# Two-layer encoder trunk on one core: the gate halves' spacing in V's weight tiles, and the ninth weight tile's role at the end of V

## The chip, the core and the metric

The kernel runs on one core of one Trainium2 chip. The metric is the device time of one execution in microseconds (us); of several runs the median is given. TensorE is called PE in the profile, its weight loads PEld, VectorE DVE, ScalarE ACT, GpSimd POOL and the engine that issues most transfers SP.

## What is computed

A sequence of 256 tokens plus 16 meta tokens (272 columns here, 1024 features) goes through two layers. Each has a token mixer (a gated recurrence in layer 0, a convolution module in layer 1) and then the part that takes nearly all the time, a PEER channel mixer:

```python
def peer_block(xc, w_query, sub_keys, expert_u, expert_v):
    ...
    expert = idx1 * PEER_N_KEYS + idx2          # 16 experts of 16384 for each head and token
    g = jax.nn.softmax(s.astype(jnp.float32), axis=-1).astype(xc.dtype)
    u = expert_u[expert]
    act = jax.nn.gelu(jnp.einsum('chkd,cd->chk', u, xc))
    v = expert_v[expert]
    return jnp.einsum('chk,chkd->cd', g * act, v)
```

After each mixer stands a layer norm. All of it is in float32.

## The kernel before

Most tokens take the PEER mixer densely: all 16384 experts are computed for them, as 128 tiles of 128 experts, and gates that are zero for experts not chosen weight the result. A stage "U" makes the activations (240 columns), a stage "V" multiplies the gated activations with the 128 tiles of `peer_v` and adds them up in eight PSUM banks `acc0` to `acc7`, one for each 128 features. V works on n = 208 columns in layer 0 and n = 192 in layer 1. The few other tokens draw single rows of the tables by indirect transfers (`rows`) in the background.

To keep float32 precision, each operand is split into a high part `hi` in a shorter format and the rest `lo`. For a tile of V, SP loads 512 KB (`raw<-peer_v`), ACT makes `hi` (line 154), DVE makes `lo` (line 161), and PE multiplies. The gates of four tiles (`JG = 4`) are split into one tile `w` by `weights`: ACT writes the high half, DVE the low half (lines 270 and 273). In it the two halves of one tile's gates lie side by side, each `T0` = 272 numbers wide, of which the first n are used. So one matmul with the weights `hi` takes both halves in one instruction (line 771: n columns, a jump, n columns, 416 or 384 in all), and one with the weights `lo` takes the high half alone (line 775). A full tile has eight of each. Two `w` tiles alternate; in the built program they begin at bytes 60640 and 69344 of each partition, both 224 above a multiple of 256.

The last four of the 128 tiles of V come as four half tiles, so that the norm after V can begin on the first 512 features while the others are still multiplied. `halves(q, h)` loads the columns of half h of two tiles (two transfers of 256 KB) and splits them. `finish_block(b)` finishes the features of bank b, and needs `halves(0, 0)` and `halves(1, 0)` for banks 0 to 3, `halves(0, 1)` and `halves(1, 1)` for banks 4 to 7. In layer 0 it is called by `collect`, which also norms, in layer 1 by `finish`, which writes the output. `take` (lines 841 and 842) adds the banks' first part to the residual `xr` on DVE.

Nine weight tiles of 4 KB per partition are shared by everything: four for `raw`, two for `hi`, two for `lo`, and a ninth, `spare`. `stream` decides who gets it by the flag `self.fifth`: where that is true, every fifth `raw` goes into it (five load tiles, two `hi`); where it is false, every third `hi` does (four load tiles, three `hi`). `u_store` sets it to true, and `peer` to false just before the half tiles. A tile can be written again once its last reader is done.

The order on each engine is set at build time by a scheduler that follows the waits of the program: an instruction that needs no buffer to come free can be placed ahead of one written earlier that does. At run time each engine, and SP's queue, works strictly in that order.

## Time and profile before

| | us |
|---|---|
| median of 3 runs | 1774.01 (1772.1 to 1779.39) |
| the profiled execution | 1777.1 |
| its span, first to last instruction | 1775.3 |
| PE busy | 1724.0 (97%) |
| DVE busy | 1511.7 (85%) |
| ACT busy | 901.1 (51%) |
| POOL busy | 625.0 (35%) |

The stage V of layer 0 runs from about 546 to 862 us of the span, its norm to about 888; V of layer 1 runs from about 1442 to 1740, and its four half tiles and the output to the end. In a view of the profile in order of time (the timeline), a row has the start and the time of a run of equal instructions, the engine, the line, what is written from what, how many, and in brackets how long the engine was idle before and what released it. The windows view gives, for each stretch, the engines' busy time, the clock granted to TensorE as a share of full speed, the share of busy DMA engines and GB/s.

### The profile page before, as it was taken

Reading aid. Unit: us, or ns where it says so; the run is one execution under the profiler, and the core shown is the slowest. Engines: PE = TensorE matmul, PEld = TensorE weight load, DVE = VectorE, ACT = ScalarE, POOL = GpSimd, SP = SyncE. Lnnn points to the kernel's source line nnn. Section 1 sums busy time; section 2 is a strip of 40 time slices with the busy share of each in tenths; the row PEclk is TensorE's granted clock in tenths of the full one; section 3 lists DMA queues with packets and bytes.
Section 4 is the critical chain, followed back from the end, with each engine's and each line's share of the span. In section 5 each row is a group of like instructions: output and inputs, shape, how many; then the busy total and the mean of one; then the engine's idle time right before and its main releaser. Section 6 shows DMA issues by size and latency. Waiting matters only on the chain.

```text
span 1775.3 us, 34693 instructions
## 1 busy us (share of the span) xinstructions
PE 1724.0 (97%) x13436; PEld 1676.6 (94%) x13436; DVE 1511.7 (85%) x2821; ACT 901.1 (51%) x1489; POOL 625.0 (35%) x424
## 2 busy tenths in 40 slices
PE   8999999999999999999998999999999999999995
PEld 7899999999999999999887899999999999999995
DVE  7786998899997889887799769978898978889865
ACT  6554444544445555885432645455444455555551
POOL 1101992111202556752000017922113137677300
PEclk9999999999999999999999999999999999999997
DMA  5545668866657999999441366579666679999982
GB/s 202 166 144 167 191 206 274 300 211 203 222 185 267 338 350 351 356 360 317 149 153 50 107 196 172 194 260 319 222 198 222 194 221 328 347 344 352 342 285 84
DMA packets 126022, 423.83 MB, mean 239 GB/s; under 512 B 20768, under 2 KB 21920, under 8 KB 125728
## 3 DMA queue, kind: packets, MB, share of 16 engines
q1 hardware_dynamic: 96272, 324.04, 55.3%
q0 software_dynamic: 29584, 97.58, 15.0%
q8 instruction: 105, 1.72, 0.4%
q14 instruction: 61, 0.50, 0.1%
HBM read 411.35 MB, written 10.20 MB: 237 GB/s over the span
## 4 chain that ended last, share of the span: by engine, by line
PE 78%; DVE 11%; DMA 4%; issue 3%; POOL 2%; ACT 2%; POOLq 0%; DVEq 0%; SPq 0%; ACTq 0%
PE u L189 42%; PE acc L771 17%; PE acc L775 11%; DMA rows<-peer_v,ids 4%; PE u L225 3%; DVE cy L1279 2%; DVE odd L1279 2%; DVE lo L161 1%; PE g L696 1%; PE g L697 1%; PE sps L587 1%; PE acc L810 1%; ACT hi L154 1%; DMA own<-own 1%; DVE x L372 1%
## 5 line engine op out<-in xcount | busy, mean ns | idle before, releaser
L154 ACT ACTIVATE hi<-raw 128x1024 fp32r<-128x1024 f32 x556 | 588.4, 1060 | 570.6 <-PE acc L771 211.5
L161 DVE TENSOR_TENSOR lo<-raw,hi 128x1024 fp32r<-128x1024 f32 x488 | 595.2, 1223 | 149.2 <-ACT hi L154 140.6
L189 PE MATMUL u<-xs,hi 128*128 128x240 f32 (+2 forms) x4544 | 568.7, 277 | 2.0 <-ACT hi L154 1.4
L189 PEld LDWEIGHTS u<-xs,hi 128*128 128x128 f32 x4544 | 537.5, 189 | 3.1 <-ACT hi L154 1.6
L771 PE MATMUL acc<-w,hi 128*128 128x416 f32 (+1 forms) x1984 | 410.6, 349 | 1.8 <-DVE w L273 1.8
L771 PEld LDWEIGHTS acc<-w,hi 128*128 128x128 f32 x1984 | 348.0, 189 | 3.5 <-DVE w L273 2.2
L1064 POOL DMA_INDIRECT rows<-peer_v,ids x128 | 206.5, 1613 | 320.8 <-DVE few_out L1105 170.2
L189 PE MATMUL u<-xs,lo 128*128 128x240 f32 (+2 forms) x2272 | 308.2, 276 | 4.1 <-POOL lo L161 3.4
L189 PEld LDWEIGHTS u<-xs,lo 128*128 128x128 f32 x2272 | 280.6, 189 | 6.1 <-POOL lo L161 5.0
L775 PEld LDWEIGHTS acc<-w,lo 128*128 128x128 f32 x2048 | 267.1, 192 | 10.3 <-DVE lo L161 8.5
L775 PE MATMUL acc<-w,lo 128*128 128x208 f32 (+1 forms) x2048 | 270.0, 273 | 6.0 <-DVE lo L161 3.5
L161 POOL TENSOR_TENSOR lo<-raw,hi 128x1024 fp32r<-128x1024 f32 x68 | 176.8, 2616 | 103.1 <-ACT hi L154 62.2
L1105 DVE SCALAR_TENSOR_TENSOR few_out<-rows,act,few_out 128x1024 f32<-128x1024 f32 x120 | 153.7, 1281 | 18.5 <-DMA rows<-peer_v,ids 18.0
L1064 POOL DMA_INDIRECT rows<-u_rows,ids x48 | 61.4, 1280 | 178.5 <-DVE rows L1071 138.8
L1081 POOL DMA_INDIRECT act<-own,turn x80 | 111.1, 1389 | 27.5 <-issue 18.6
L225 PE MATMUL u<-x,raw 128*128 128x272 f32 x480 | 114.2, 398 | 5.0 <-DMA x<-h 5.0
L225 PEld LDWEIGHTS u<-x,raw 128*128 128x128 f32 x480 | 92.6, 193 | 24.4 <-DMA raw<-w_in 5.0
L703 ACT ACTIVATE act_b<-g 128x488 f32<-128x488 f32 (+39 forms) x50 | 19.4, 388 | 123.7 <-DVE act_b L665 97.2
L380 POOL TENSOR_SCALAR xs<-x,par 128x272 fp32r<-128x272 f32 (+1 forms) x4 | 3.5, 877 | 186.0 <-DVE x L372 186.0
L1071 DVE SCALAR_TENSOR_TENSOR rows<-rows,wide 128x1024 f32<-128x1024 f32 x48 | 58.5, 1218 | 3.7 <-DMA rows<-u_rows,ids 3.7
L678 DVE TENSOR_TENSOR AB<-iota,iT 128x2048 f16<-128x2048 f16 x50 | 60.7, 1217 | 0.0
L752 POOL COPY own<-act_b 128x512 f32<-128x512 f32 (+2 forms) x15 | 15.0, 1005 | 121.9 <-ACT act_b L714 95.3
(281 smaller groups left out, 1803.2 us busy)
## 6 DMA issues: line engine op xcount, KB each, us to landing
raw<-peer_u SPq DMA_DIRECT2D x256, 512.0 KB
raw<-peer_v SPq DMA_DIRECT2D x248, 512.0 KB
raw<-w_query SPq DMA_DIRECT2D x28, 512.0 KB
raw<-pw SPq DMA_DIRECT2D x22, 512.0 KB
raw<-w_in SPq DMA_DIRECT2D x16, 512.0 KB
raw<-w_out SPq DMA_DIRECT2D x8, 512.0 KB
raw<-peer_v SPq DMA_DIRECT2D x16, 256.0 KB
own<-own POOLq DMA_DIRECT2D x15, 256.0 KB
```

Of the source, the lines that this page charges most:

```text
L154: self.act_hi = nc.scalar.activation(hi, raw, AF.Copy).ins
L161: i = e.tensor_tensor(lo[:, s], raw[:, s], hi[:, s].bitcast(F32), op=OP.subtract)
L189: self.mm = nc.tensor.matmul(ps[:, :n], l[:, k, :], xs(k, r)[:, :n], start=start, stop=stop)
L225: self.mm = self.nc.tensor.matmul(ps[:, :n], raw[:, k, :], x[:, k, :n], start=k == 0, stop=k == NB - 1)
L678: nc.vector.tensor_tensor(AB.rearrange("p x c (a b) -> p (x c) a b", b=2), keys, iT[:, c0 // HC].rearrange("p x c b -> p (x c) b")[:, :, N ...
L771: self.mm = nc.tensor.matmul(acc[b][:, :2 * n].rearrange("p (a t) -> p a t", a=2), hi, w[:, :, :n], start=j == 0, stop=j == NK - JG - 1, s ...
L775: self.mm = nc.tensor.matmul(main[b][:, :n], hi if p_ else lo, w[:, i, :n], start=False, stop=j == NK - 1 and not p_, skip_group_check=True)
L1064: self.last_rows = self.nc.gpsimd.indirect_dma_start(out=t, out_offset=None, in_=table, in_offset=bass.IndirectOffsetOnAxis(ap=few["ids"][ ...
L1071: self.nc.vector.scalar_tensor_tensor(t, t, 1.0, few["x"], op0=OP.mult, op1=OP.mult, accum_out=few["act"][:, k:k + 1])
L1081: self.nc.gpsimd.indirect_dma_start(out=few["act"][:, k:k + 1], out_offset=None, in_=few["table"].rearrange("p j (t o) -> (p j t) o", o=1) ...
L1105: nc.vector.scalar_tensor_tensor(few["out"], t, w, few["out"], op0=OP.mult, op1=OP.add)
L1279: nc.vector.scalar_tensor_tensor(z, h, w, z, op0=OP.mult, op1=OP.add)
```

## The change

The halves of a `w` tile lie 256 numbers apart instead of 272, so a jump of 1024 bytes instead of 1088 leads from the first column of one half to that of the other, and 2048 instead of 2176 bytes from one of the four tiles' gates to the next. The tile keeps its size and place. And the flag `self.fifth` is no longer set to false before the half tiles. In layer 0 `collect` sets it to false at its last block, when no half tile is left to load; in layer 1 it stays true to the end.

```diff
+WROW = 256
...
                 def weights(j0, count):
-                    t = self.xp.tile([P, JG, 2, T0], F32R, tag="xs", name="w")
+                    t = self.xp.tile([P, JG * 2 * T0], F32R, tag="xs", name="w")
+                    t = t[:, :JG * 2 * WROW].rearrange("p (j a n) -> p j a n", j=JG, a=2)
...
-                self.fifth = False
                 halves(0, 0)
...
     def collect(self, sp, acc, y, n):
...
         for b in range(NB):
+            self.fifth = b < NB - 1
             finish_block(b)
```

No engine gets more or fewer instructions, and the order on PE and POOL stays as it was. The order on SP, ACT and DVE changes at the half tiles alone. Lines after the added ones are higher by one or two in the changed kernel.

SP's queue at the end of V in layer 1, before. The numbers tell buffers apart: `raw_21198` and `raw_21220` are the last two full tiles, `raw_21245` is `halves(0, 0)`, `raw_21293` is `halves(1, 0)`, `raw_21340` is `halves(0, 1)` and `raw_21371` is `halves(1, 1)`; `gb` are the gains and biases of the last norm (1 MB):

```order
L144 DMA raw_21198<-peer_v 128x1024
L144 DMA raw_21220<-peer_v 128x1024
L144 DMA raw_21245<-peer_v 128x512 x2
L144 DMA raw_21293<-peer_v 128x512 x2
L1304 DMA gb_21257<-gb 128x2048
L144 DMA raw_21340<-peer_v 128x512 x2
L144 DMA raw_21371<-peer_v 128x512 x2
```

The same place of SP's queue in the changed kernel:

```order
L145 DMA raw_21198<-peer_v 128x1024
L145 DMA raw_21220<-peer_v 128x1024
L145 DMA raw_21245<-peer_v 128x512 x2
L145 DMA raw_21293<-peer_v 128x512 x2
L145 DMA raw_21340<-peer_v 128x512 x2
L1306 DMA gb_21257<-gb 128x2048
L145 DMA raw_21371<-peer_v 128x512 x2
```

The load of the third half tile has moved ahead of `gb`, since it has a fifth load tile to go into.

ACT at the same place, the `hi` of the same tiles, before:

```order
L154 ACTIVATE hi_21200<-raw_21198 128x1024
L154 ACTIVATE hi_21222<-raw_21220 128x1024
L154 ACTIVATE hi_21343<-raw_21340 128x1024
L154 ACTIVATE hi_21248<-raw_21245 128x1024
L154 ACTIVATE hi_21296<-raw_21293 128x1024
L154 ACTIVATE hi_21374<-raw_21371 128x1024
```

ACT in the changed kernel:

```order
L155 ACTIVATE hi_21200<-raw_21198 128x1024
L155 ACTIVATE hi_21222<-raw_21220 128x1024
L155 ACTIVATE hi_21248<-raw_21245 128x1024
L155 ACTIVATE hi_21296<-raw_21293 128x1024
L155 ACTIVATE hi_21343<-raw_21340 128x1024
L155 ACTIVATE hi_21374<-raw_21371 128x1024
```

Before, the third half tile had the spare tile for its `hi` and stood ahead of the first two; now it has moved behind them, and the four stand in the order in which they are needed.

ACT at the end of V in layer 0, before. Here `hi_10657` is the last full tile, `hi_10683` is `halves(0, 0)`, `hi_10737` is `halves(1, 0)`, `hi_10812` is `halves(0, 1)` and `hi_10843` is `halves(1, 1)`; `shift`, `sq` and `pre_x` belong to the norm:

```order
L154 ACTIVATE hi_10657<-raw_10655 128x1024
L154 ACTIVATE hi_10737<-raw_10734 128x1024
L154 ACTIVATE hi_10683<-raw_10680 128x1024
L154 ACTIVATE hi_10812<-raw_10809 128x1024
L154 ACTIVATE hi_10843<-raw_10840 128x1024
L864 ACTIVATE shift_10700<-shift_10768 128x272
```

ACT in the changed kernel:

```order
L155 ACTIVATE hi_10657<-raw_10655 128x1024
L155 ACTIVATE hi_10683<-raw_10680 128x1024
L155 ACTIVATE hi_10737<-raw_10734 128x1024
L155 ACTIVATE hi_10812<-raw_10809 128x1024
L866 ACTIVATE shift_10700<-shift_10768 128x272
L887 ACTIVATE sq_10790<-x1_10692 128x272
L889 ACTIVATE pre_x_10693<-x1_10692,par_72 128x272
L887 ACTIVATE sq_10794<-x1_10692 128x272
L889 ACTIVATE pre_x_10693<-x1_10692,par_72 128x272
L887 ACTIVATE sq_10798<-x1_10692 128x272
L889 ACTIVATE pre_x_10693<-x1_10692,par_72 128x272
L155 ACTIVATE hi_10843<-raw_10840 128x1024
```

The first half tile has moved ahead of the second, and the fourth behind the norm's `shift` and its first three squares. On DVE the `lo` of that fourth half tile has moved back by three operations of the norm.

## The prediction

> **What bounds the kernel now.** I read the page first, then the windows of the two V stages, then the timeline of PE, ACT, DVE and SP around the half tiles, and last the starts of PE's matmuls in undisturbed stretches. The page names PE:

> ```profile
> PE 1724.0 (97%) x13436; PEld 1676.6 (94%) x13436; DVE 1511.7 (85%) x2821; ACT 901.1 (51%) x1489; POOL 625.0 (35%) x424
> ```

> The change touches V alone. Its two stages, without their first tiles in layer 0 (columns: PE, PEld, DVE, ACT and POOL busy, clock, DMA share, GB/s):

> ```profile
> 568.00:842.00 274.00, 269.16 (x1793) 264.09 (x1792) 237.81 (x258) 173.18 (x266) 153.87 (x100) 1.00 0.95 345
> 1442.00:1742.00 300.00, 297.29 (x2060) 296.93 (x2058) 244.10 (x268) 157.72 (x164) 160.09 (x110) 1.00 0.91 322
> ```

> In layer 0 PE is idle 274 - 269.16 = 4.8 us, with the transfer engines 95% busy: PE and transfers bind together. In layer 1 PE is idle 2.7 us, most of it at the very end (below), and the transfers have more room: PE binds. So a quicker matmul pays fully in layer 1 and less surely in layer 0, and a slower one is partly taken up by the idle time of layer 0. The instructions in question are these (by form):

> ```profile
> L771 PE MATMUL acc<-w,hi 128*128 128x416 f32 x992 | 209.8, 353 | 0.9 <-DVE w L273 0.9
> L771 PE MATMUL acc<-w,hi 128*128 128x384 f32 x992 | 200.8, 344 | 0.9 <-DVE w L273 0.9
> ```

> Those means are latencies of pipelined instructions; the price of one is the distance from start to start.

> **Part 1, the end of V in layer 1.** PE, from the `lo` matmuls of the last tile but one on:

> ```profile
> 1736.85 1.04 PE L775 MATMUL acc<-w,lo 128*128 128x192 f32 x8
> 1737.72 1.60 PE L771 MATMUL acc<-w,hi 128*128 128x384 f32 x8
> 1739.15 1.03 PE L775 MATMUL acc<-w,lo 128*128 128x192 f32 x8
> 1744.08 3.70 PE L775 MATMUL acc<-w,hi 128*128 128x192 f32 x16 [3.90 <-DVE xr L842]
> ```

> Eight matmuls with `lo` last 1737.72 - 1736.85 = 0.87, so PE could go on at 1739.15 + 0.87 = 1740.02. It goes on at 1744.08: 4.06 us are lost. ACT and DVE at that time:

> ```profile
> 1734.69 1.06 ACT L154 ACTIVATE hi<-raw 128x1024 fp32r<-128x1024 f32 x1 [1.25 <-PE acc L771]
> 1740.41 2.95 ACT L154 ACTIVATE hi<-raw 128x1024 fp32r<-128x1024 f32 x3 [4.67 <-DMA raw<-peer_v]
> ```

> ```profile
> 1735.78 1.22 DVE L161 TENSOR_TENSOR lo<-raw,hi 128x1024 fp32r<-128x1024 f32 x1 [1.08 <-ACT hi L154]
> 1742.45 1.22 DVE L161 TENSOR_TENSOR lo<-raw,hi 128x1024 fp32r<-128x1024 f32 x1 [5.44 <-ACT hi L154]
> 1743.59 1.14 DVE L842 TENSOR_TENSOR xr<-xr,acc 128x192 f32<-128x192 f32 x4
> ```

> And SP's issues, from two questions on short stretches:

> ```profile
> 1727.70 3.16 SPq L144 DMA_DIRECT2D raw<-peer_v  x4
> ...
> 1733.28 0.33 SPq L1304 DMA_DIRECT2D gb<-gb  x1
> 1734.73 3.11 SPq L144 DMA_DIRECT2D raw<-peer_v  x4
> ```

> By the order, the first of ACT's three at 1740.41 is the third half tile. Its load was issued at 1734.73, behind 1 MB of `gb`, and landed 5.7 us later. The loads of the first two half tiles were issued from 1727.70 on; by the same 5.7 us they were there by 1733.4 or little later. So ACT, in strict order, waited for data that nobody needed yet, with data behind it that PE needed. DVE's `lo` starts at 1742.45, when the second of the three is done; `xr`, which PE waits for, stands behind that `lo`. In the changed order the first half tile's `hi` is next on ACT. Its buffer is that of the last tile but one, free when the `hi` matmuls of that tile end at 1736.85. So `hi` runs from 1736.9 to 1737.9, `lo` to 1739.2, the first `xr` of four is done 0.3 us later, and PE is free only at 1740.02. The wait goes. Next in line are the second half tile's `lo` (its `hi` needs the last full tile's, free at 1739.15; its `lo` then follows the four `xr`, to about 1741.6) and PE needs it only after 24 matmuls, at 1742.8. The third load goes out one `lo` earlier, when its fifth tile allows, and ahead of `gb`; the last, behind `gb`, is needed only when the third has been multiplied, which ended 12 us after the first began (1744.08 to 1756.08).

> The wait has a second price. The granted clock, in the idle time, in the first 24 matmuls after it, and in the same 24 matmuls of the third half tile:

> ```profile
> 1740.19:1744.08 3.89, 0.00 (x0) 0.91 0.12 43
> 1744.08:1749.29 5.21, 5.21 (x24) 0.50 0.00 0
> 1753.34:1756.08 2.74, 2.74 (x28) 1.00 0.00 0
> ```

> At half clock they took 5.21, at full clock 2.74: 2.47 us more. Without the idle time the clock has no reason to fall. Part 1 is -(4.06 + 2.47) = -6.5 us. Bounds: -7.0, if the few matmuls after 1749.29 gain too (DVE hides that, I take it), and -2, if half of the wait comes back and the clock falls all the same.

> **Part 2, the end of V in layer 0.** There the hoisted half tile was the second, and its data were there, so the cost was small:

> ```profile
> 861.77 2.12 PE L775 MATMUL acc<-w,hi 128*128 128x208 f32 x16 [0.40 <-DVE xr L842]
> ...
> 874.04 0.48 PE L775 MATMUL acc<-w,lo 128*128 128x208 f32 x2 [1.13 <-DVE lo L161]
> ```

> ```profile
> 863.93 1.06 ACT L154 ACTIVATE hi<-raw 128x1024 fp32r<-128x1024 f32 x1 [2.33 <-PE acc L775]
> ...
> 871.88 0.51 ACT L887 ACTIVATE pre_x<-x,par 128x272 f32<-128x272 f32 x1
> ```

> ```profile
> 872.77 1.22 DVE L161 TENSOR_TENSOR lo<-raw,hi 128x1024 fp32r<-128x1024 f32 x1
> ...
> 874.61 0.43 DVE L872 TENSOR_TENSOR total<-total,rest 128x272 f32<-128x272 f32 x1
> ```

> With the first half tile first, its `lo` and the DVE work behind it start about one `hi` earlier (1.0 us), and the 0.40 goes. Against it, the fourth half tile's `hi`, at 863.93 so far, moves behind the `pre_x` of 871.88, to 872.4, and its `lo` on DVE behind three operations of 0.35 each, so that PE's 1.13 would grow by 1.0. The two nearly cancel: 0, with -0.8 and +1.0 as bounds.

> **Part 3, the spacing.** Neither ACT's nor DVE's instructions for `w` change in count or size, and they stand beside PE's work. What can change is PE's pace. Layer 1, two neighbouring tiles, and one tile of layer 0:

> ```profile
> 1599.12 1.60 PE L771 MATMUL acc<-w,hi 128*128 128x384 f32 x8
> 1600.56 1.04 PE L775 MATMUL acc<-w,lo 128*128 128x192 f32 x8
> 1601.43 1.65 PE L771 MATMUL acc<-w,hi 128*128 128x384 f32 x8
> 1602.91 1.04 PE L775 MATMUL acc<-w,lo 128*128 128x192 f32 x8
> ```

> ```profile
> 569.90 1.70 PE L771 MATMUL acc<-w,hi 128*128 128x416 f32 x8
> 571.43 1.04 PE L775 MATMUL acc<-w,lo 128*128 128x208 f32 x8
> ```

> The same work takes 1.44 us in one tile of layer 1 and 1.48 in the next, and so on in turn: 180 and 185 ns a matmul. The two differ only in where their gates lie (2176 bytes on, 128 above a multiple of 256). So where the halves lie does cost something. In layer 0 one takes 1.53 / 8 = 191 ns. What a matmul without a jump takes, from two rows of the chain that ended last:

> ```profile
> 55.10 27.50 PE u L225 x120
> ...
> 100.15 3.01 PE u L189 x24
> ```

> The first are float32 matmuls of 272 columns that stand as two records each, 229 ns a record; taken as two passes over the columns (an estimate), 0.421 ns a column. The second, in the short format of V, take 125.4 for 272, 10.8 above that pace. By that pace 416 columns are 175.3 and 384 are 161.8, so V's matmuls are 16 above it in layer 0, 18 and 23 in layer 1. The jump from the end of one half to the next is now 1088 - 832 = 256 bytes in layer 0 and 320 in layer 1; it becomes 192 and 256. I take the jump of 256, the one whose cost is lowest, as the good case: then all tiles of layer 1 cost what the better ones do, 62 tiles x 0.04 = -2.5 us (bounds: +2.5, all like the worse ones, and -9.8, all at 10.8 above the pace). Layer 0 loses its good case and pays 18 to 23 instead of 16: +2 to +7 us on 992 matmuls. I take +2, since the idle 4.8 us take up the first of it. Bounds -5.2 (at 10.8) and +7.

> [...]

> **Sum.** -6.5 + 0 - 2.5 + 2.0 = -7.0 us. The profiled execution (1777.1, span 1775.3) would come to 1770.1; it lies 3.1 us above the median, so for the median 1774.0 - 7.0 = 1767.0.

> **The rivals.**
> - *The spacing does nothing*: the odd and even tiles then differ by something that stays. 1774.0 - 6.5 = 1767.5. For it: it changes no count; against it: the alternation itself.
> - *The spacing is the larger gain*: both layers come down to 10.8 above the pace, 9.8 us in layer 1 (992 x 9.9 ns) and up to 5.2 in layer 0, where the transfers may hold it. With Part 1, 1752.5 to 1757.7, say 1755. For it: all halves then begin alike, 224 above a multiple of 256; against it: that is where the slower tiles of layer 1 have their first half.
> - *Slower: the halves 1024 bytes apart hinder the reading*, by a further step like that from 18 to 23, so 28 in both layers: 12 x 992 = 11.9 in layer 0, less the idle 4.8, and 7.5 x 992 = 7.4 in layer 1, less 6.5: +8, 1782. It decides from 6.5 us / 1984 = 3.3 ns a matmul on. For it only the slower tiles, against it that layer 0 shows nothing above 16.
> - *The wait in layer 1 half comes back*, since DVE's `lo` and `xr` or the third load are late next: with 2 us of it left, the gain is 2.1, or 4.5 if the clock stays full, and the time with Part 3 1771.4 or 1769.0. [...]

> **How the numbers follow.** Chances: the forecast 0.37, the spacing without effect 0.16, the larger gain 0.24, the half repair 0.13, slower 0.10. A change under 0.5% (8.9 us) can hardly be told from none. Faster than 1765.1: all of the larger gain, two fifths of the forecast, a little of the second: 0.42. Slower than 1782.9: half of the last, 0.05. The rest, 0.53, is within. The range from 1756 to 1776 leaves out half of the larger gain and most of the slower case. The forecast's own range is 1763 to 1771.

> **What would show it.** Part 1: PE's idle time before the first half tile at the end of layer 1 under 0.5 us, no stretch of half clock there, ACT's four `hi` one by one and the first at about 3 us before the last full tile's end. Part 2: the wait for `xr` gone, the one for `lo` near 2 us or shifted, the norm starting within 1 us of where it did. Part 3: all tiles of layer 1 alike, at 2.31 from start to start, and layer 0's eight at 1.55. I am wrong if the pace of both layers moves the same way by more than 3 ns a matmul, or if PE still waits 2 us or more at 1740.

## The result, and the profile after

The changed kernel takes 1763.22 us (median of 12 runs, 1760.31 to 1767.85), the kernel before 1773.53 (12 runs, 1767.01 to 1779.39). The ratio is 0.9947 [0.9935, 0.9958] (the interval of 95% in brackets), 9.4 us less. Measured a second time, beside the experiments, it is 0.9964 [0.995, 0.9977], 6.4 us less. The ratios are taken over all the runs and are not those of the medians, which lie 10.3 us apart the first time and 8.0 the second; where this document gives a gain in us beside a ratio, it is the ratio's. The forecast of -7.0 lies between the two ratios and is smaller than both differences of the medians; the interval of the second measurement (4.1 to 8.9 us) has it, that of the first (7.4 to 11.5) does not. The prediction held that a change under 0.5% (8.9 us) can hardly be told from none: the first measurement is beyond that, the second short of it, and neither interval reaches zero. The profiled execution of the changed kernel took 1761.52, with a span of 1759.8. That is 15.5 us below the span of the profile before, so the two profiles lie further apart than the medians.

The page's line on the engines, and the windows of the two V stages (columns as before: PE, PEld, DVE, ACT and POOL busy, clock, DMA share, GB/s):

```profile
PE 1716.6 (98%) x13436; PEld 1671.8 (95%) x13436; DVE 1512.1 (86%) x2821; ACT 901.4 (51%) x1489; POOL 625.5 (36%) x424
```

```profile
568.00:842.00 274.00, 272.40 (x1818) 269.36 (x1817) 240.74 (x261) 176.91 (x273) 150.21 (x100) 1.00 0.95 347
1442.00:1738.00 296.00, 295.49 (x2089) 295.32 (x2088) 247.60 (x275) 155.60 (x158) 160.12 (x108) 1.00 0.91 324
```

PE is busy 7.4 us less in all (1724.0 to 1716.6), and in layer 1 it is idle only 0.5 us in a window that reaches into the half tiles.

**The end of V in layer 1.** The timeline of PE, from the last full tile on, and of ACT and DVE at that time:

```profile
1728.81 1.59 PE L772 MATMUL acc<-w,hi 128*128 128x384 f32 x8
1730.23 1.03 PE L776 MATMUL acc<-w,lo 128*128 128x192 f32 x8
1731.10 1.98 PE L776 MATMUL acc<-w,hi 128*128 128x192 f32 x16
...
1733.81 0.61 PE L776 MATMUL acc<-w,hi 128*128 128x192 f32 x4
```

```profile
1728.13 1.06 ACT L155 ACTIVATE hi<-raw 128x1024 fp32r<-128x1024 f32 x1 [1.24 <-PE acc L772]
1730.43 1.06 ACT L155 ACTIVATE hi<-raw 128x1024 fp32r<-128x1024 f32 x1 [1.23 <-PE acc L772]
```

```profile
1729.23 1.23 DVE L162 TENSOR_TENSOR lo<-raw,hi 128x1024 fp32r<-128x1024 f32 x1 [1.07 <-ACT hi L155]
1730.52 1.15 DVE L843 TENSOR_TENSOR xr<-xr,acc 128x192 f32<-128x192 f32 x4
```

ACT makes the half tiles' `hi` one by one; the row of three with 4.67 us of idle time ahead of it is gone. The first starts at 1728.13, just when the `hi` matmuls of the last full tile but one have ended. `xr` starts at 1730.52 and PE goes on at 1731.10 without a gap. The first 24 matmuls of the half tiles take 1733.81 - 1731.10 = 2.71 us, not 5.21: the clock stays full (1.00 granted from 1730.23 to 1745.5, where before it was 0.50 in those 24). From the first matmul of the last full tile to the end of the span there are 1759.8 - 1728.81 = 31.0 us; before, 1775.3 - 1737.72 = 37.6. That is -6.6.

**The tiles.** Two tiles of layer 1, and one of layer 0:

```profile
1599.10 1.59 PE L772 MATMUL acc<-w,hi 128*128 128x384 f32 x8
1600.52 1.03 PE L776 MATMUL acc<-w,lo 128*128 128x192 f32 x8
1601.39 1.59 PE L772 MATMUL acc<-w,hi 128*128 128x384 f32 x8
1602.82 1.03 PE L776 MATMUL acc<-w,lo 128*128 128x192 f32 x8
```

```profile
569.35 1.70 PE L772 MATMUL acc<-w,hi 128*128 128x416 f32 x8
570.88 1.04 PE L776 MATMUL acc<-w,lo 128*128 128x208 f32 x8
```

In layer 1 all tiles are alike now, 1.42 to 1.43 for the eight and 2.29 from tile to tile; before they took 2.31 and 2.36 in turn. By the medians of the starts it is 2.293 against 2.311 and 2.356. In layer 0 the median goes from 2.405 to 2.413.

**The end of V in layer 0.** PE before, at two places that the prediction did not show:

```profile
868.44 0.70 PE L863 MATMUL shift<-total,fours 128*128 128x272 f32 x2 [1.65 <-issue]
...
874.36 2.01 PE L897 MATMUL var<-sq,ones 128*128 128x272 f32 x8
```

PE after, then the fourth half tile's `hi` on ACT and its `lo` on DVE:

```profile
863.44 0.70 PE L865 MATMUL shift<-total,fours 128*128 128x272 f32 x2 [1.73 <-issue]
...
864.63 3.29 PE L776 MATMUL acc<-w,hi 128*128 128x208 f32 x16
...
870.24 0.48 PE L776 MATMUL acc<-w,lo 128*128 128x208 f32 x2 [0.69 <-DVE lo L162]
870.55 2.01 PE L899 MATMUL var<-sq,ones 128*128 128x272 f32 x8
```

```profile
867.30 1.04 ACT L155 ACTIVATE hi<-raw 128x1024 fp32r<-128x1024 f32 x1
```

```profile
868.96 1.22 DVE L162 TENSOR_TENSOR lo<-raw,hi 128x1024 fp32r<-128x1024 f32 x1
```

The fourth `hi` stands behind three `pre_x`, as the order said, and its `lo` comes 5.52 us after `shift` instead of 4.33 (872.77 - 868.44). From `shift` to the first `var` matmul it is 7.11 instead of 5.92. `shift` itself comes a little earlier, 7.57 us behind the start of the last full tile's `lo` matmuls instead of 8.11. From that start to the norm's row of 24 `pre` matmuls it is 23.68 instead of 23.01 (855.87 to 879.55 and 860.33 to 883.34), so the end of layer 0 as a whole takes 0.7 us more. And the 16 `hi` matmuls at 864.63 take 3.29 where the same 16 took 1.95 before: a stretch of half clock that was not there before (its windows stand in the last section).

### The profile page after: what moved, and what is told of

Read it like the earlier page. It is cut to its first block, busy times and chain, and to the rows that moved or that the text cites. A ratio compares the mean times of both kernels' runs of the same rounds, so it can differ in the third digit from the quotient of the medians.

```text
span 1759.8 us, 34693 instructions
## 1 busy us (share of the span) xinstructions
PE 1716.6 (98%) x13436; PEld 1671.8 (95%) x13436; DVE 1512.1 (86%) x2821; ACT 901.4 (51%) x1489; POOL 625.5 (36%) x424
## 4 chain that ended last, share of the span: by engine, by line
PE 40%; DVE 8%; DMA 1%; issue 1%; ACT 1%; POOL 1%; POOLq 0%; ACTq 0%; DVEq 0%
PE u L190 20%; PE acc L772 11%; PE acc L776 7%; DVE cy L1281 2%; DVE odd L1281 2%; DMA rows<-peer_v,ids 1%; DMA own<-own 1%; DVE lo L162 1%; PE g L697 0%; PE g L698 0%; PE sps L588 0%; PE acc L812 0%; DVE x L373 0%; DVE x L337 0%; PE var L899 0%
## 5 line engine op out<-in xcount | busy, mean ns | idle before, releaser
L1107 DVE SCALAR_TENSOR_TENSOR few_out<-rows,act,few_out 128x1024 f32<-128x1024 f32 x120 | 153.7, 1281 | 13.4 <-DMA rows<-peer_v,ids 13.1
```

The costliest lines, as they stand in the source:

```text
L1107: nc.vector.scalar_tensor_tensor(few["out"], t, w, few["out"], op0=OP.mult, op1=OP.add)
```

## The experiments

### The two parts apart

The spacing alone, on the kernel before:

```diff
+WROW = 256
...
-                    t = self.xp.tile([P, JG, 2, T0], F32R, tag="xs", name="w")
+                    t = self.xp.tile([P, JG * 2 * T0], F32R, tag="xs", name="w")
+                    t = t[:, :JG * 2 * WROW].rearrange("p (j a n) -> p j a n", j=JG, a=2)
```

> The kernel before with halves 256 numbers apart and nothing else. Theory A (two separate gains: the spacing sets the pace of PE, the order on ACT the end of layer 1): layer 1's tiles all at 2.29 us from start to start as in the changed kernel, layer 0's at 2.41, the wait of about 3.9 us and the half clock at the end of layer 1 still there; time 3 to 4.5 us under before. Rival B (the flag alone does it, the pace follows from the fifth load tile): no change of pace, 0 us.

Measured: 1770.72 us against 1771.98, ratio 0.9993 [0.9977, 1.0008]. The pace is that of the changed kernel in both layers, but the end of layer 1 keeps its wait and its half clock:

```profile
1731.21 1.03 PE L776 MATMUL acc<-w,lo 128*128 128x192 f32 x8
1737.35 3.70 PE L776 MATMUL acc<-w,hi 128*128 128x192 f32 x16 [5.11 <-DVE xr L844]
```

```profile
1733.68 2.95 ACT L155 ACTIVATE hi<-raw 128x1024 fp32r<-128x1024 f32 x3 [5.80 <-DMA raw<-peer_v]
```

The wait is longer than before (5.11 against 3.90): PE comes to the end earlier, but the third half tile's data, which ACT waits for, come no earlier by as much: ACT's three begin 2.47 us after the start of PE's last full `lo` row (1733.68 - 1731.21), before 1.26 (1740.41 - 1739.15). The granted clock is 0.50 from 1736.17 to 1742.99. A part of what the tiles gained is given back there.

The flag alone, on the kernel before:

```diff
-                self.fifth = False
                 halves(0, 0)
...
+            self.fifth = b < NB - 1
             finish_block(b)
```

> The kernel before with the flag left true to the last half tile of V, halves 272 apart. Theory A: pace as before (2.31 and 2.36 in turn in layer 1, 2.40 in layer 0), the wait for xr at the end of layer 1 and the half clock gone, 6.5 us less there, the norm after layer 0's V 0.7 us later at most; time 5.5 to 6.7 us under before. Rival B: all of the 10.3 us. Rival C (layer 0's shorter waits in the changed kernel, 5 us in its profile, come from the flag): V of layer 0 shorter by several us here as well.

Measured: 1767.61 us, ratio 0.9976 [0.9963, 0.9988], 4.2 us less. The pace is as before; PE at the end of layer 1:

```profile
1737.51 1.98 PE L775 MATMUL acc<-w,hi 128*128 128x192 f32 x16
```

No idle time stands behind the row, and the 16 take 1.98 instead of 3.70: no wait, no half clock. So the two parts act where the prediction placed them. Of the two alone the flag is worth more, 4.2 us [2.1, 6.6] against 1.2 [-1.4, 4.1].

### What in the flag cures the wait

The flag does three things at the end of layer 1: ACT's order changes, the third load goes ahead of `gb`, and it has a fifth load tile. Here only the order is changed: the flag stays false before the half tiles, and each `hi` of the four half tiles may not be issued ahead of the `hi` written before it.

```diff
-            with self.tc.issue_after(self.last_diag) if self.last_diag else nullcontext():
+            with self.tc.issue_after(self.last_diag) if self.last_diag else nullcontext(), \
+                    self.tc.issue_after(self.act_hi) if self.chain else nullcontext():
```

> The kernel before, with ACT told to make the four half tiles' hi in the order in which they are written; the flag stays false, so the third load stays behind gb and the third hi keeps the spare tile. Theory A1 (ACT's order makes the wait): PE idle under 0.5 us before the first half tile of layer 1, no half clock, 6.5 us less as with the flag. Rival A2 (the earlier load of the third half tile, in its fifth tile and ahead of gb, is needed): most of the 3.9 us stay, because the data still land at the same time; less than 3 us gained. In layer 0 the fourth half tile's hi stays early: by A1 the end there is 0.4 to 1 us better than before.

Measured: 1766.89 us, ratio 0.997 [0.9956, 0.9985]. PE:

```profile
1738.19 1.98 PE L776 MATMUL acc<-w,hi 128*128 128x192 f32 x16
```

The wait and the half clock are gone here too, with the third load behind `gb` as before and four load tiles. So ACT's order alone made the wait: an instruction that was placed early because its buffer was free, and whose data came last, held up the two behind it. The earlier load is not needed for that.

### What in the spacing costs

The prediction took the jump from the end of one half to the start of the next as the cost. In this kernel there is none: the changed kernel with the halves directly one behind the other.

```diff
-                    t = t[:, :JG * 2 * WROW].rearrange("p (j a n) -> p j a n", j=JG, a=2)
+                    t = t[:, :JG * 2 * n].rearrange("p (j a n) -> p j a n", j=JG, a=2)
```

> The changed kernel with the halves directly behind each other (n numbers apart, no jump). Theory D (what a matmul over both halves pays above a plain one is the jump, and one of a whole 256 bytes is as good as none): layer 1 as in the changed kernel, 1.42 us for eight, layer 0 down from 1.53 to 1.49 (186 ns each), time 3 to 5 us under the changed kernel unless transfers hold layer 0. Rival E (the place of the halves against 256 bytes counts, not the jump): layer 1 alike or better, layer 0, whose second halves begin 64 bytes on, no better than before, 1.51 to 1.53. Rival F: equal spacing by a power of two was the gain; layer 0 and 1 both slower than in the changed kernel.

Measured: 1763.56 us, ratio 0.9946 [0.9928, 0.9964], as the changed kernel. One tile of layer 1 and one of layer 0:

```profile
1600.54 1.59 PE L772 MATMUL acc<-w,hi 128*128 128x384 f32 x8
1601.96 1.03 PE L776 MATMUL acc<-w,lo 128*128 128x192 f32 x8
```

```profile
569.79 1.68 PE L772 MATMUL acc<-w,hi 128*128 128x416 f32 x8
571.30 1.04 PE L776 MATMUL acc<-w,lo 128*128 128x208 f32 x8
```

Without any jump the eight matmuls take 1.426 in layer 1 (median of all tiles), exactly as with a jump of 256 bytes, and 1.527 in layer 0, exactly as with the old jump of 256 bytes. In these two pairs a jump as such costs nothing (1.426 and 1.426, 1.527 and 1.527); some of the layouts cost something, up to 1.48 in the old layer 1 (with the jump, the places where the halves begin change as well).

Which ones, a sweep in one kernel was to tell: 15 pairs of a jump and a place of the first half, in turn from one `w` tile to the next. It is one profiled execution (1764.99 us beside 1775.43 for the kernel before).

```diff
+                    gap, at = SWEEP[j0 // JG % len(SWEEP)]
-                    t = t[:, :JG * 2 * WROW].rearrange("p (j a n) -> p j a n", j=JG, a=2)
+                    t = t[:, at:at + JG * 2 * (n + gap)].rearrange("p (j a n) -> p j a n", j=JG, a=2)
```

> The changed kernel with another distance and start of the halves for each group of four tiles, fifteen pairs in turn in each layer (gap behind the first half of 0, 16, 32, 64, 128, 192, 256 bytes; start 224, 0, 96 or 224 above a multiple of 256 bytes). Read from the trace alone: eight matmuls with hi of one tile, start to start. Theory D (the gap alone): 1.42 in layer 1 and 1.49 in layer 0 with gaps of 0 and 256, more in between, whatever the start. Rival E (where a half begins against 256 bytes): the same gap at another start moves it by as much as another gap does. Rival G (16 or 64 byte lines): only the gap of 16 and those at a start of 0 stand out.

The time of the eight two-half matmuls in us, from their starts, medians over some eight tiles each (twelve in the first row), for nine of the 15 settings:

| jump (bytes) | first half's place | layer 0 | layer 1 |
|---|---|---|---|
| 0 | as before | 1.528 | 1.426 |
| 64 | as before | 1.530 | 1.435 |
| 128 | as before | 1.536 | 1.416 |
| 192 | as before | 1.534 (the changed kernel) | 1.411 |
| 256 | as before | 1.523 (the kernel before) | 1.426 (the changed kernel) |
| 0 | 32 bytes on | 1.514 | 1.428 |
| 64 | 32 bytes on | 1.524 | 1.441 |
| 128 | 32 bytes on | 1.552 | 1.410 |
| 192 | 32 bytes on | 1.517 | 1.422 |

All 15 settings lie between 1.514 and 1.552 in layer 0 and between 1.410 and 1.441 in layer 1. The old layout of layer 1 (a jump of 320 bytes) was, with 1.44 and 1.48 in turn, at and above the upper end of that range, and 256 bytes are about its middle. No simple rule on the jump orders the table. The place counts as much as the jump: 32 bytes on take layer 0 from 1.528 to 1.514 with a jump of 0, and from 1.536 to 1.552 with one of 128. And what is the best in one layer is the worst in the other (128 bytes, 32 bytes on). Single tiles of one setting differ too, in layer 0 with a jump of 128 from 1.515 to 1.542. Why is open.

### The sweep's best places, and the order alone with the new spacing

Two kernels with ACT's order forced as above and the flag false: one with the halves 256 numbers apart, the other with the places that the sweep found quick (every `w` tile used from 32 bytes on, halves 256 numbers apart in layer 0 and 224 in layer 1).

```diff
+                    row = 256 if n == 208 else 224
+                    t = t[:, 8:8 + JG * 2 * row].rearrange("p (j a n) -> p j a n", j=JG, a=2)
```

> Both parts at once, but with the wait cured by ACT's order alone: the four half tiles' hi stand on ACT in written order in both layers, the flag is false before the half tiles as in the kernel before, the halves of w lie 256 apart. Theory (the cure is ACT's order; the fourth half tile's hi behind three pre_x costs 1.2 us at the end of layer 0, from shift to the first square product 7.1 instead of 5.9): V as in the changed kernel (2.41 and 2.293 a tile), end of layer 1 without a wait, 6.2 us from shift to the first square product; about 1 us less than the changed kernel, so 9 to 11 us less than before. Rival (the earlier load and the fifth load tile are worth something of their own): 2 us or more above the changed kernel.

> As e6, but with the places that were best in the sweep: every tile of w starts 32 bytes later (on a multiple of 256), halves 256 numbers apart in layer 0 and 224 in layer 1. Theory (what counts is where the two halves start, and by 1 per cent of the eight matmuls at most): eight matmuls 1.517 us in layer 0 and 1.410 in layer 1, against 1.534 and 1.426; 124 tiles each, so 2.0 us less in layer 1 and 0 to 2.1 less in layer 0 than e6, where the transfers bind too. Rival (the sweep's medians of eight tiles are scatter): no difference to e6.

Measured: 1763.46 us, ratio 0.9952 [0.9934, 0.997], with 256 in both; 1760.15 us, ratio 0.9938 [0.992, 0.9955], with the sweep's places. One tile of layer 1 of the latter:

```profile
1600.47 1.57 PE L772 MATMUL acc<-w,hi 128*128 128x384 f32 x8
1601.88 1.03 PE L776 MATMUL acc<-w,lo 128*128 128x192 f32 x8
```

By medians of all tiles the eight take 1.411 and 1.517, as the sweep had it (1.410 and 1.517), so its small medians were no scatter. From tile to tile that is 2.280 and 2.393 against 2.293 and 2.413. The kernel with both is the fastest of all, 11.0 us below the kernel before (13.4 by the medians); the intervals of the last two overlap, so the places' own worth, 3.3 us by the medians, is not proved by the times. The first of the two stays 2.1 us below the changed kernel by the medians (1765.51, its second measurement), where about 1 was expected; their intervals overlap too.

The end of layer 0 in the kernel with the order and 256, and in the changed kernel as profiled a second time (below):

```profile
866.57 0.70 PE L868 MATMUL shift<-total,fours 128*128 128x272 f32 x2 [1.73 <-issue]
...
872.49 2.01 PE L902 MATMUL var<-sq,ones 128*128 128x272 f32 x8
```

```profile
867.76 0.70 PE L865 MATMUL shift<-total,fours 128*128 128x272 f32 x2 [1.73 <-issue]
...
874.86 2.01 PE L899 MATMUL var<-sq,ones 128*128 128x272 f32 x8
```

5.92 us from `shift` to `var` where the fourth `hi` stays early, 7.10 where it stands behind three `pre_x`. This second execution of the changed kernel has no half clock there and still takes 7.10, so the 1.2 us are the fourth `hi`, not the clock.

### The changed kernel and the spacing alone, once more

Apart the parts gave 1.2 and 4.2 us, both in one kernel 9.4. The changed kernel and the spacing alone were measured again, on one chip.

> The changed kernel itself once more, beside the parts on one chip. First measured 0.9947 [0.9935, 0.9958] of the kernel before, 9.4 us, where the two parts apart gave 1.2 and 4.2. If the parts add up and the difference is scatter: 5 to 7 us below before here, and near the sum of e9 and the flag's part. If the two help each other (the matmuls' gain in layer 1 is given back at the end as long as the wait stands there): 8 us or more again.

> The spacing alone once more (kernel before, halves 256 apart). First 0.9993 [0.9977, 1.0008]. If the spacing's gain in layer 1 (4.3 us of pace) is really there but partly given back at the end of layer 1, where the half tiles' data land when they did before: 1 to 4 us below before, and the wait at the end longer than in the kernel before by what PE came earlier (5.4 instead of 4.2). If it is worth nothing: 1.000.

Measured: the changed kernel 1765.51 us, 0.9964 [0.995, 0.9977]; the spacing alone 1771.0, 0.9994 [0.9977, 1.0011]. The first measurement was the more favourable of two; with the second, the sum of the parts (5.3) and the whole (6.4) differ by less than their intervals. Whether the two help each other the times do not settle: the second interval (4.1 to 8.9) has the expected sum as well as the 8 us of the other case. For the spacing alone the time cannot be told from none (1.1 us). The wait at the end is longer than before, as expected, but by 0.5 us (4.43 where the kernel before has 3.90) and not by 1.2.

There is a second place where the quicker pace is lost. First and last start of the two-half matmuls in V of layer 1 (a group's view of that line; after the count stand the shortest, median and longest duration in ns), for the kernel before, the flag alone, the changed kernel, its second profile, and the spacing alone twice:

```profile
L771 PE MATMUL acc<-w,hi x992: 334/343/442, 1444.1 to 1739.0; 128*128 128x384 f32 x199
L771 PE MATMUL acc<-w,hi x992: 334/343/445, 1441.6 to 1736.5; 128*128 128x384 f32 x199
L772 PE MATMUL acc<-w,hi x992: 334/334/440, 1439.5 to 1730.1; 128*128 128x384 f32 x199
L772 PE MATMUL acc<-w,hi x992: 331/334/443, 1443.0 to 1735.7; 128*128 128x384 f32 x199
L772 PE MATMUL acc<-w,hi x992: 334/334/443, 1438.7 to 1731.0; 128*128 128x384 f32 x199
L772 PE MATMUL acc<-w,hi x992: 334/334/442, 1440.5 to 1733.4; 128*128 128x384 f32 x199
```

The stage takes 294.9 and 294.9 with the old spacing, and 290.6, 292.7, 292.3 and 292.9 with the new one, though the pace is the same in these four. The shortest is the changed kernel's first profile. In the other three PE waits once or twice between 1463 and 1480, some 10 to 15 tiles into the stage, as in the second profile of the changed kernel:

```profile
1475.17 1.59 PE L772 MATMUL acc<-w,hi 128*128 128x384 f32 x8
1476.60 1.09 PE L776 MATMUL acc<-w,lo 128*128 128x192 f32 x8
1479.20 1.69 PE L772 MATMUL acc<-w,hi 128*128 128x384 f32 x8 [1.51 <-issue]
```

The pace is worth 123 x (2.3335 - 2.293) = 5.0 us in this stage (2.3335 is the mean of the old 2.311 and 2.356), and this wait takes some 2 of them in three of these four profiles. The three other kernels with new places (halves joined, order and 256, sweep's places) wait near there as well, for 0.8, 1.6 and 0.6 us. With the old spacing no profile has it.

PE waits for its weights there. Of the rows below, the first is ACT's in the same profile: `hi` ends at 1478.10 + 1.06 = 1479.16, and PE goes on at 1479.20. The second is PE's in the second profile of the spacing alone, which names DVE's `lo`:

```profile
1478.10 1.06 ACT L155 ACTIVATE hi<-raw 128x1024 fp32r<-128x1024 f32 x1 [4.03 <-PE acc L776]
```

```profile
1476.26 1.14 PE L776 MATMUL acc<-w,lo 128*128 128x192 f32 x8 [1.52 <-DVE lo L162]
```

Why ACT and DVE, idle themselves, are late there is not settled. The `lo` matmuls that the first row names had ended by 1477.69 (1476.60 + 1.09). A late load of `raw` is a candidate; no run tests it.

## Why the prediction was right

The sum was -7.0, the two measurements -9.4 and -6.4. By its steps:

- **Part 1**, -6.5: the trace shows -6.6, and the experiment on ACT's order confirms the chain that the prediction read (third `hi` first, data late, `lo` and `xr` behind it). The two halves of the term, the 4.06 us and the 2.47 of the half clock, both came back in full. The flag alone is worth 4.2 [2.1, 6.6] us by the times; 6.6 is at the edge of that, and Part 2 takes 0.7 of it, which leaves 5.9.
- **Part 2**, 0 with -0.8 and +1.0: mis-sized, though within its bounds. With the wait for `xr` gone, `shift` comes 8.11 - 7.57 = 0.5 earlier, but the late fourth `hi` cost 7.11 - 5.92 = 1.2, so +0.7. The prediction said that the two nearly cancel, because it set the first half tile's earlier `lo` (1.0) against the later fourth one. The first gives only 0.5, since PE then waits 1.73 ahead of `shift` where it waited 1.65.
- **Part 3, layer 1**, -2.5: the sign was right, the reason for the size was not. It was to come from the slower half of the tiles alone, which should fall to the better ones' 2.311; in fact all fell to 2.293, worth 5.0 us, twice the term. Then a new wait early in the stage took some 2 us, and the four stages together are 294.9 - 292.1 = 2.8 shorter on average. The term came out right by two errors that cancel, which is luck. The half that was not foreseen, that a faster PE runs into something else early in the stage, is the kind of question that the prediction asked for layer 0 only.
- **Part 3, layer 0**, +2: mis-sized. The pace is slower by 0.008 us a tile, 1 us over the stage. What was taken as the good case (a jump of 256 bytes) is not special: the table has 0 bytes at nearly the same cost and two settings below it, one of which came out the same again (1.517 against 1.527). The stage's length, 308 to 312 us in all profiles, varies more from execution to execution, by waits for `lo` and `turn`, than the spacing moves it: from first to last start it is 310.9 on average in the three profiles with the old layout and 309.1 in the five with halves 256 apart, so a loss of 2 does not show.

So the largest term was right in mechanism and in size. That the other three, -0.5 in the forecast, came near in sum owes something to luck: the pieces above give +0.7 and -2.8, with nothing seen for layer 0.

That the place of the gates makes a difference, as the prediction read from its two tiles (1.44 against 1.48), the table shows: 1.410 to 1.441 in layer 1 by jump and place alone, and the two layouts tried again came out the same (1.411 and 1.517). Whether another engine has part in it, no run here shows.

Of the rivals, "the spacing does nothing" and "slower" fell with the pace in layer 1. "The larger gain", 10.8 ns above the column pace in both layers, was half right on layer 1: from the fourth of the eight on, the matmuls there come every 173 ns, 161.8 + 11.2 (161.8 is the prediction's estimate for 384 columns, from the 229 ns of a float32 record; no run shows the two passes that it takes such a record for), but the first three are slower (202, 176 and 182 ns), and the pace gained 5.0 us instead of its 9.8. It failed on layer 0, where they come every 192 on average. "Half of the wait comes back" did not happen.

## What to carry to other kernels

An instruction that a scheduler places early because its buffer is free must also have its data early; on an engine that works in strict order, as ACT here, a hoisted instruction whose transfer comes last holds up what stands behind it (PE lost 4.06 us by it), and a constraint on the order cured that here without any buffer (no idle time ahead of the half tiles). Take the price of a layout from a sweep within one kernel (15 settings in one profiled run here), since settings differed by up to 2.5% without a visible rule. And a gain in pace is worth its full sum only up to the next stretch where something else is late (here some 2 of 5.0 us went there): look for such a stretch in the same stage, not only at its end.

## What the hardware showed unexpectedly

The clock went down after less idle time than the 3.90 us of the gap that the prediction read. At the end of layer 0 PE is idle 1.73 us ahead of `shift` in the changed kernel. In its profile and in that of the kernel before, the changes of the granted clock lie whole multiples of 3.4133 us apart within each (the shortest distance is 3.413, one of them, the longest 959.145, 281 of them). Windows of 3.41 us, laid so that they end where the granted clock changes, for the changed kernel and for the kernel with ACT's order alone, then the same place in the kernel before and in the one with the order and 256 (first the busy time of PE, at the end the clock; the boundaries of the latter two are whole steps of 3.413 us from another change of the clock in the same execution):

```profile
861.55:864.96 3.41, 1.68 (x13) 1.47 (x12) 2.89 (x7) 0.40 (x1) 0.00 (x0) 1.00 0.46 159
864.96:868.37 3.41, 3.41 (x19) 3.41 (x17) 3.38 (x11) 3.26 (x7) 0.00 (x0) 0.50 0.05 17
```

```profile
865.44:868.86 3.42, 1.70 (x14) 1.47 (x13) 2.90 (x6) 0.40 (x1) 0.00 (x0) 1.00 0.45 159
868.86:872.27 3.41, 3.41 (x18) 3.41 (x18) 3.41 (x11) 2.31 (x7) 0.00 (x0) 0.50 0.12 46
```

```profile
866.18:869.59 3.41, 1.76 (x14) 1.54 (x13) 2.89 (x6) 0.40 (x1) 0.00 (x0) 1.00 0.53 138
869.59:873.01 3.42, 3.33 (x30) 3.15 (x29) 3.42 (x11) 2.31 (x6) 0.00 (x0) 1.00 0.17 63
```

```profile
864.88:868.29 3.41, 1.72 (x13) 1.67 (x14) 2.89 (x8) 0.48 (x2) 0.00 (x0) 1.00 0.50 169
868.29:871.70 3.41, 2.75 (x25) 2.58 (x24) 3.41 (x9) 2.23 (x6) 0.00 (x0) 1.00 0.00 1
```
